# An encoder layer on one core: copy-outs moved to ScalarE, the last pair's stores moved to another queue, and the closing norm rearranged

## The chip, the cores and the metric

The kernel runs on one core of one Trainium2 chip. The metric is the device time in microseconds (us) of one execution. The kernel before was timed three times: 1658.04, 1663.20 and 1662.12 us, median 1662.12. One more execution was taken with the profiler; it lasted 1666.81 us.

## The reference, cut to what matters

One inference step of a one-layer encoder over 1024 prompt rows and 8 x 16 sample rows, D_MODEL = 1024, D_FF = 3072, all in float32. Two attention branches are merged and projected, and a gated MLP with a causal depthwise convolution of width 3 follows; RMSNorm stands before and after each of the two. The change touches the MLP alone:

```python
def conv_ffn(h, conv_buf, w_upg, conv_w, conv_b, w_down):
    u, g = jnp.split(h @ w_upg, 2, axis=-1)
    upad = jnp.concatenate([conv_buf, u], axis=1)
    c = conv_b
    for tap in range(CONV_WIDTH):
        c = c + conv_w[tap] * upad[:, tap:tap + s]
    y = (jax.nn.gelu(c, approximate=True) * g) @ w_down
    return y, upad[:, -(CONV_WIDTH - 1):]

f, conv_new = conv_ffn(rmsnorm(x, g_pre_ffn), conv_buf, w_upg, conv_w, conv_b, w_down)
x = x + rmsnorm(f, g_post_ffn)
```

rmsnorm(f, g) is f times the inverse root of the mean square of its row (plus a small constant), times the gain g of each column.

## The kernel before, in words

The 1152 rows lie in nine blocks of 128 (NT = 9). Every float32 matmul is made of three matmuls in float32r: each operand is split into a high part (a ScalarE copy, line 1007 for up weights, 1292 for the down stage) and the rest (a VectorE subtraction, lines 1008 and 1293). Around these, both stages multiply in the Strassen-Winograd way: seven products of half-sized operands in place of eight, whose results are summed in PSUM and on VectorE.

**The up stage.** There are 24 pairs f (NF = 24), each one tile of 128 u columns with its tile of g columns. The left operands of a pair are formed from its raw weights `uw` by `left_factors`; the right operands b11, b21, t3, t2, t1, b22 and t4 are tiles that stay in SBUF for the whole stage. Every product is two chunks of 288 columns (CW), 12 matmuls each, in two PSUM banks. For the first five pairs (NH = 5) the products with b11 and b21 ran ahead (`head_away`), and their results went to DRAM as a_dr and c_dr. `tail` does the rest of a pair: zb takes the product with t3, then xb the one with t2; xb is copied out into u2; the product with t1 is summed onto xb, which is copied out into u4; the product with b22 is summed onto it and xb is copied out a third time, into rows of u; last zb takes the product with t4. Since the next product is summed onto the same banks, TensorE waits for each copy-out, chunk by chunk. `take` (line 1140) is the copy-out. In the pairs run ahead a PSUM bank holds only the part made here, and `take` adds `a`, loaded back from a_dr, on VectorE (line 1144); in the others it is a ScalarE copy (line 1146). The rows of u that ran ahead are loaded from c_dr (line 1192). The convolution begins with one ScalarE instruction for each piece (line 1183: 448 columns, 128 sample columns, and 576 for the other half), then two on VectorE each (line 1185), then gelu on ScalarE (line 1187). GpSimd copies the new convolution state (lines 1202, 1203) and multiplies with the gate (1204, 1209); four stores bring the result to z_dr[f] (lines 1205, 1206, 1210, 1211). After the last pair the collected state is stored as conv_new (line 1247).

**Order of work.** A planner orders each engine's instructions by a model of their times, first those that come earlier in the program; each engine then runs its queue in that order, and an instruction that waits holds those behind it. All DMAs but none of the compute instructions stand in SyncE's queue (SP). Only where `tc.manual_schedule` names an engine is its order that of the program text.

**Memory between the stages.** The up stage's right-hand pools are uraw (the raw weights, two tiles of 8 KB a partition), b11 (18 KB), and further on t3, t2, t1, b22 and t4. The down stage lays its pools over them in the order in which they are opened: zp0 (9 KB) and wp0 (8 KB) come first and so lie over uraw, za0 and wb0 (8 KB each) over b11. zp and wp take raw loads from z_dr and w_down, za and wb the split operands. A tile waits for the last use of what it covers.

**The down stage.** The 24 tiles z_dr are multiplied with w_down in two groups g of six pairs of tiles. The first product, p2, uses the tiles of the upper half: z12 and wd12 in zp0 and wp0, then z14, z16. The sample block's columns go first in each product (p20s), with their own split (line 1299 and 1300). The sums stand in yacc, nine blocks of 1024 columns in two halves. In the second group the order at the end is written out by hand for VectorE: for each of the nine blocks the last 18 matmuls, `add_to` (line 1366) of the second half, and `finish`, a generator: x1 is loaded, ScalarE squares the block's yt and sums the squares (line 1401), GpSimd scales the sum and raises it to the power -1/2 (lines 96, 97), and, one block later, VectorE multiplies yt with that and with the gain gpo (line 1407), adds x1 (line 1410) and SyncE stores y. The ninth block is done in two halves; its two sums are added on GpSimd (line 1403), and its first half's last addition is on GpSimd.

Of the kernel before, what the change touches and what calls it, by code (L numbers as in the profile page):

```python
# [13 lines left out]
AF = mybir.ActivationFunctionType  # L14
# [4 lines left out]
P = 128  # L19
# [33 lines left out]
def encoder_step(ctx, tc, x, w_in, w_o, w_out, w_upg, w_down, kc, vc, state_conv, conv_w, conv_b,  # L53
# [40 lines left out]
    def rstd_of(ss, out, eng=nc.vector):  # L94

        eng.tensor_scalar(out, ss, 1.0 / D, EPS, op0=ALU.mult, op1=ALU.add)
        nc.gpsimd.tensor_tensor(out, out, nhalf[:, 0:out.shape[1]], op=ALU.pow)
# [986 lines left out]
    with ExitStack() as ph:  # L1084
# [55 lines left out]
        def take(xb, a, yb, out):  # L1140

            for c in range(2):
                if yb is None:
                    nc.vector.tensor_tensor(out[c], xb[c], a[c], op=ALU.add)  # L1144
                else:
                    nc.scalar.activation(out[c], xb[c], AF.Copy)
            return out

        def tail(f, ops, xb, a, yb, forms):
            zb = banks(psz, f"z{f}")  # L1150
            product(zb, next(ops), of("t3"), True, False)
            product(xb, next(ops), of("t2"), yb is None, False)
            next(forms, None)
            w = r1[f % 2].tile([P, 4 * 3 * 256], F32, name=f"w{f}", tag="act")
            u = w[:, 0:UT]
            us = u[:, UP:UT].rearrange("p (b q) -> p b q", b=NSB)
            gg = w[:, UT:UT + T].rearrange("p (h c n) -> p h c n", h=2, c=2)
            u2 = take(xb, a, yb, [w[:, UT + T + c * CW:UT + T + (c + 1) * CW] for c in range(2)])
            nc.gpsimd.memset(u[:, 0:2], 0.0)
            product(xb, next(ops), of("t1"), False, False)  # L1160
            next(forms, None)
            if "wk" not in work:
                work["wk"] = r1[2].tile([P, 4 * 3 * 256], F32, name="wk", tag="act")
                work["st"] = r1[3].tile([P, 4 * 3 * 256], F32, name="st", tag="act")
                nc.sync.dma_start(work["st"][:, 0:NF * NSB * 2].rearrange("p (f b q) -> p f b q", f=NF, b=NSB), state_conv)
            wk, st = work["wk"], work["st"]
            scv = st[:, 0:NF * NSB * 2].rearrange("p (f b q) -> p f b q", f=NF, b=NSB)
            cnew = st[:, NF * 16:NF * 34].rearrange("p (f n) -> p f n", f=NF)
            nc.gpsimd.tensor_copy(us[:, :, 0:2], scv[:, f])
            u4 = take(xb, a, yb, [wk[:, 2304 + c * CW:2304 + (c + 1) * CW] for c in range(2)])  # L1170
            for c in range(2):
                nc.vector.tensor_tensor(gg[:, 1, c], zb[c], u4[c], op=ALU.add)

            def conv(h):

# [12 lines left out]
                return c  # L1188

            for dst, c, cols, samples in rows(u, us):  # L1190
                if yb is None:
                    nc.sync.dma_start(dst, by_sample(c_dr[f][:, c, cols], samples))
                else:
                    nc.vector.tensor_tensor(dst, by_sample(yb[c][:, cols], samples), by_sample(a[c][:, cols], samples),
                                            op=ALU.add)
            c1 = conv(0)
            product(xb, next(ops), of("b22"), False, True)
            next(forms, None)
            take(xb, a, yb, [u[:, 2 + H1 + c * CW:2 + H1 + (c + 1) * CW] for c in range(2)])
            c2 = conv(1)  # L1200
            product(zb, next(ops), of("t4"), False, True)
            nc.gpsimd.tensor_copy(cnew[:, f, 0:2], u[:, SEQ:SEQ + 2])
            nc.gpsimd.tensor_copy(cnew[:, f, 2:].rearrange("p (b q) -> p b q", b=NSB), us[:, :, SS:SS + 2])
            nc.gpsimd.tensor_tensor(c2, c2, gg[:, 1].rearrange("p c n -> p (c n)"), op=ALU.mult)
            nc.sync.dma_start(z_dr[f][:, H1:512], c2[:, 0:512 - H1])
            nc.sync.dma_start(z_dr[f][:, 512 + P:T], c2[:, 512 - H1:])
            for c in range(2):
                nc.vector.tensor_tensor(gg[:, 0, c], zb[c], u2[c], op=ALU.add)
            nc.gpsimd.tensor_tensor(c1, c1, gg[:, 0].rearrange("p c n -> p (c n)"), op=ALU.mult)
            nc.sync.dma_start(z_dr[f][:, 0:H1], c1[:, 0:H1])  # L1210
            nc.sync.dma_start(z_dr[f][:, 512:512 + P], c1[:, H1:])

        def right_factors():

# [29 lines left out]
        for f in range(NF):  # L1244
            tail(f, *(head_back(f) if f < NH else head(f)), forms)
        cnew = work["st"][:, NF * 16:NF * 34].rearrange("p (f n) -> p f n", f=NF)
        nc.sync.dma_start(conv_new, cnew)
    xo_stack.close()
    r1_stack.close()

# [3 lines left out]
    with ExitStack() as ph:  # L1254
# [3 lines left out]
        def right(name):  # L1258
            return ph.enter_context(tc.tile_pool(name=name, bufs=1, side="right", reuse_waits="tile"))

        zp, wp, za, wb = [None] * 6, [None] * 6, [], []
        for q in range(3):
            zp[q], wp[q] = right(f"zp{q}"), right(f"wp{q}")
            za.append(right(f"za{q}"))
            wb.append(right(f"wb{q}"))
            if q == 0:
                yacc = right("yacc").tile([P, NT, 2, 512], F32, name="yacc")
        zsp = [right(f"zs{i}") for i in range(6)]
        for q in range(3, 6):
# [119 lines left out]
        def finish(tb, n):  # L1389

            if n % 2 == 0:
                pool = (wp + zp[3:])[3 + n // 2]
                box["x1"] = pool.tile([P, 2, D], F32, name=f"x1f{n}", tag="r")
            x1 = box["x1"][:, n % 2]
            nc.sync.dma_start(x1, x1_dr[tb][:])
            st = tp.tile([P, 4], F32, name=f"stf{tb}", tag="stf")
            sq = box["sq"][:, n % 2]
            yt = yacc[:, tb].rearrange("p a b -> p (a b)")
            parts = [slice(0, 512), slice(512, D)] if n == NT - 1 else [slice(0, D)]
            for i, c in enumerate(parts):  # L1400
                nc.scalar.activation(sq[:, c], yt[:, c], AF.Square, accum_out=st[:, i:i + 1])
            if len(parts) > 1:
                nc.gpsimd.tensor_tensor(st[:, 0:1], st[:, 0:1], st[:, 1:2], op=ALU.add)
            rstd_of(st[:, 0:1], st[:, 2:3], nc.gpsimd)
            yield
            for i, c in enumerate(parts):
                nc.vector.scalar_tensor_tensor(yt[:, c], yt[:, c], st[:, 2:3], gpo[:, c], op0=ALU.mult, op1=ALU.mult)  # L1407
            for i, c in enumerate(parts):
                eng = nc.gpsimd if n == NT - 1 and i == 0 else nc.vector
                eng.tensor_tensor(yt[:, c], yt[:, c], x1[:, c], op=ALU.add)  # L1410
                nc.sync.dma_start(y[tb][:, c], yt[:, c])

        box = {}
        pending = []

        def start_finish(tb):
            ends = finish(tb, box.setdefault("n", 0))
            box["n"] += 1
            next(ends)
            for e in pending:  # L1420
                next(e, None)
            pending[:] = [ends]

        for g in range(2):
# [44 lines left out]
            p3, n, _ = stepper("p3", pairs, xb, ex, False, False, True)  # L1469
            box["sq"] = zp[5].tile([P, 2, D], F32, name="sqf", tag="r")  # L1470
            with tc.manual_schedule(engines={mybir.EngineType.DVE}):
                add_to(xb[0], 4, 1, g, False)
                start_finish(4)
                for step, j, ps, tb in ((p5, 1, xb[1], 5), (p3, -1, ex, NT - 1), (p3, 0, xb[0], 0), (p5, 2, xb[2], 6),
                                        (p3, 1, xb[1], 1), (p5, 3, xb[3], 7), (p3, 2, xb[2], 2), (p3, 3, xb[3], 3)):
                    for i in range(n):
                        step(i, j)
                    add_to(ps, tb, 1, g, False)
                    start_finish(tb)
                for e in pending:  # L1480
                    next(e, None)

# [85 lines left out]
```

## Time and profile before

| | |
|---|---|
| timed runs, us | 1658.04, 1662.12, 1663.20 |
| profiled execution, us | 1666.81 |
| its span, first to last instruction, us | 1665.0 |
| mean granted TensorE clock | 0.991 |
| TensorE matmul, busy us | 1609.2 (97%) |
| VectorE (DVE), busy us | 1086.8 (65%) |
| ScalarE (ACT), busy us | 726.6 (44%) |
| GpSimd (POOL), busy us | 223.8 (13%) |
| DMA over SyncE's queue | 204.69 MB, 36.2% of 16 engines |

The span is what lies between the first and the last instruction; some 1.8 us of the execution lie outside. An engine is idle before an instruction when something that it needs is late; the profile names in brackets how long and what came last (the releaser). The granted clock is a share of TensorE's full 2.4 GHz. In the profile's rows PE is the matmul, PEld the weight load beside it, and a q behind an engine's name is its queue of issued DMAs or waits. The up stage runs from some 862 to 1385 us, its ahead pairs' tails until 959; the down stage follows to the end.

### The profile page before, as it was taken

The numbers are of one execution on the slowest core, as the hardware profiler recorded it, in microseconds if no ns is written. First come the engines' busy times: TensorE is split into PE (matmuls) and PEld (weight loads), VectorE is DVE, ScalarE is ACT, GpSimd is POOL, SyncE is SP. The second block draws the span as 40 slices with busy tenths as digits, with TensorE's granted clock in tenths as the row PEclk, the third lists the DMA queues.
The fourth block names the chain that finished last, engine by engine and source line by source line (L and its number), as shares of the span: only waits on it lengthen the run. The fifth ranks groups of instructions, "written<-read, shape, count | busy, mean of one in ns | idle before, by whom it ended". The sixth has DMA issues, their size and how long they took to land. (4 is left out here: it accounts for less than half of the span.)

```text
span 1665.0 us, 27771 instructions
## 1 busy us (share of the span) xinstructions
PE 1609.2 (97%) x10839; PEld 1480.8 (89%) x10839; DVE 1086.8 (65%) x2009; ACT 726.6 (44%) x1417; POOL 223.8 (13%) x297
## 2 busy tenths in 40 slices
PE   6999999999999999999999999999999998999997
PEld 6999998788888889978898999999999997888886
DVE  6965546665665546454397766766666675965986
ACT  7511235565454445332373344444444444534342
POOL 1000011111111103411002211111111110000003
PEclk9999999999999999999999999999999999999999
DMA  7743326445333236442254311221221129053023
GB/s 256 246 167 143 113 83 208 141 142 163 121 116 119 72 126 229 135 161 94 76 188 128 118 64 70 80 80 71 75 80 67 68 68 339 2 194 128 1 94 134
DMA packets 95364, 206.47 MB, mean 124 GB/s; under 512 B 21704, under 2 KB 46072, under 8 KB 95232
## 3 DMA queue, kind: packets, MB, share of 16 engines
q1 hardware_dynamic: 95232, 204.69, 36.2%
q8 instruction: 85, 1.39, 0.3%
q14 instruction: 47, 0.39, 0.1%
HBM read 148.13 MB, written 61.24 MB: 126 GB/s over the span
## 5 line engine op out<-in xcount | busy, mean ns | idle before, releaser
L143 PE MATMUL x<-xot,s 128*128 128x288 f32 x1152 | 157.7, 295 | 0.9 <-DVE w L1144 0.9
L143 PEld LDWEIGHTS x<-xot,s 128*128 128x128 f32 x1152 | 154.9, 188 | 1.1 <-ACT a L1007 1.1
L1354 PE MATMUL x<-wbp,zap 128*128 128x512 f32 x576 | 135.3, 389 | 0.0
L1354 PEld LDWEIGHTS x<-wbp,zap 128*128 128x128 f32 x576 | 108.1, 188 | 22.4
L1007 ACT ACTIVATE s<-uw 128x512 fp32r<-128x512 f32 x96 | 60.1, 626 | 96.1 <-issue 41.7
L1354 PE MATMUL p<-wbp,zap 128*128 128x512 f32 x432 | 102.0, 393 | 0.0
L1354 PEld LDWEIGHTS p<-wbp,zap 128*128 128x128 f32 x432 | 82.2, 190 | 17.2
L1008 DVE TENSOR_TENSOR s<-uw,s 128x512 fp32r<-128x512 f32 x96 | 68.9, 718 | 32.3 <-ACT s L1007 32.3
L1185 DVE SCALAR_TENSOR_TENSOR wk<-w,cw,wk 128x128 f32<-128x128 f32 (+2 forms) x144 | 83.0, 613 | 9.9 <-ACT wk L1183 9.1
L671 ACT ACTIVATE p<-p,m 128x256 f32<-128x256 f32 (+4 forms) x128 | 74.9, 588 | 33.0 <-DVE m L666 33.0
L143 PE MATMUL x<-xob,s 128*128 128x288 f32 x576 | 82.6, 299 | 6.3 <-DVE wk L1144 6.3
L143 PEld LDWEIGHTS x<-xob,s 128*128 128x128 f32 x576 | 79.6, 191 | 6.9 <-ACT s L1007 2.6
L1008 DVE TENSOR_TENSOR a<-uw,a 128x512 fp32r<-128x512 f32 x62 | 42.8, 691 | 63.6 <-ACT a L1007 62.4
L143 PE MATMUL z<-xot,s 128*128 128x288 f32 x576 | 80.7, 295 | 0.0
L143 PE MATMUL z<-xot,a 128*128 128x288 f32 x576 | 80.7, 295 | 0.0
L143 PEld LDWEIGHTS z<-xot,s 128*128 128x128 f32 x576 | 78.1, 188 | 0.0
L143 PEld LDWEIGHTS z<-xot,a 128*128 128x128 f32 x576 | 78.1, 188 | 0.0
L143 PE MATMUL ix<-t,s_i 128*128 128x288 f32 x480 | 65.6, 295 | 0.3 <-DVE iu L188 0.3
L143 PEld LDWEIGHTS ix<-t,s_i 128*128 128x128 f32 x480 | 64.3, 188 | 0.5 <-issue 0.5
L143 PE MATMUL x<-xob,a 128*128 128x288 f32 x456 | 63.9, 295 | 0.0
L143 PE MATMUL y<-xob,a 128*128 128x288 f32 x456 | 63.9, 295 | 0.0
L143 PEld LDWEIGHTS x<-xob,a 128*128 128x128 f32 x456 | 61.8, 188 | 0.0
(657 smaller groups left out, 3890.9 us busy)
## 6 DMA issues: line engine op xcount, KB each, us to landing
uw<-in_w_upg SPq DMA_DIRECT2D x53, 512.0 KB, 4.5
iw<-in_w_in SPq DMA_DIRECT2D x27, 512.0 KB, 4.6
gg<-in_dr SPq DMA_DIRECT2D x16, 576.0 KB, 3.9
in_dr<-gt SPq DMA_DIRECT2D x42, 192.0 KB, 1.9
z_dr<-wk SPq DMA_DIRECT2D x24, 256.0 KB, 2.1
z_dr<-wk SPq DMA_DIRECT2D x24, 224.0 KB, 1.9
xt<-in_x SPq DMA_DIRECT2D x9, 512.0 KB, 9.9
oT<-o_dr SPq DMA_DIRECT2D x8, 576.0 KB, 7.1
```

The lines of the kernel that those rows point to most:

```text
L143: nc.tensor.matmul(ps, w[:, i, k], right(j, c, k), start=first and n == 0, stop=last and n == len(todo) - 1, skip_group_check=True)
L671: nc.scalar.activation(p[h][:, 0:n], p[h][:, 0:n], AF.Exp, bias=least[h], scale=-1.0, accum_out=st.d[:, h, i:i + 1])
L1007: nc.scalar.activation(sp[:, 0], src, AF.Copy)
L1008: nc.vector.tensor_tensor(sp[:, 1], src, fr(sp[:, 0]), op=ALU.subtract)
L1185: nc.vector.scalar_tensor_tensor(out, src(t), cw[:, f, t:t + 1], out, op0=ALU.mult, op1=ALU.add)
L1354: nc.tensor.matmul(ps, z[:, i, k, c], w[:, j, k], start=first and n == 0, stop=last and n == 2, skip_group_check=True)
```

## The change

Five edits.

- `take` copies xb with ScalarE in every pair; in the pairs run ahead VectorE then adds `a` to the copy in SBUF.
- The four z_dr stores of the last pair, and the store of conv_new, are issued from GpSimd's queue and no longer from SyncE's.
- The pools zp0 and wp0 are opened after za0 and wb0, so that the two pairs of pools change places in memory.
- In `finish` the gain is multiplied onto yt, in place, right behind the square, in every block; mean and small constant are worked out by VectorE; GpSimd does the power alone; and one fused VectorE instruction multiplies with that and adds x1.
- `start_finish` takes the block's `add_to` as an argument. For the ninth block the first half's square and product come before that addition, and so does the end of the eighth block.

```diff
         def take(xb, a, yb, out):
             for c in range(2):
+                nc.scalar.activation(out[c], xb[c], AF.Copy)
                 if yb is None:
-                    nc.vector.tensor_tensor(out[c], xb[c], a[c], op=ALU.add)
-                else:
-                    nc.scalar.activation(out[c], xb[c], AF.Copy)
+                    nc.vector.tensor_tensor(out[c], out[c], a[c], op=ALU.add)
             return out
...
-            nc.sync.dma_start(z_dr[f][:, H1:512], c2[:, 0:512 - H1])
-            nc.sync.dma_start(z_dr[f][:, 512 + P:T], c2[:, 512 - H1:])
+            queue = nc.gpsimd if f == NF - 1 else nc.sync
+            queue.dma_start(z_dr[f][:, H1:512], c2[:, 0:512 - H1])
+            queue.dma_start(z_dr[f][:, 512 + P:T], c2[:, 512 - H1:])
...
-        nc.sync.dma_start(conv_new, cnew)
+        nc.gpsimd.dma_start(conv_new, cnew)
...
         for q in range(3):
-            zp[q], wp[q] = right(f"zp{q}"), right(f"wp{q}")
+            if q:
+                zp[q], wp[q] = right(f"zp{q}"), right(f"wp{q}")
             za.append(right(f"za{q}"))
             wb.append(right(f"wb{q}"))
             if q == 0:
+                zp[q], wp[q] = right(f"zp{q}"), right(f"wp{q}")
                 yacc = right("yacc").tile([P, NT, 2, 512], F32, name="yacc")
...
             parts = [slice(0, 512), slice(512, D)] if n == NT - 1 else [slice(0, D)]
+            if n < NT - 1:
+                yield
             for i, c in enumerate(parts):
+                if i:
+                    nc.vector.tensor_scalar(st[:, 0:1], st[:, 0:1], 1.0 / D, EPS, op0=ALU.mult, op1=ALU.add)
+                    yield
                 nc.scalar.activation(sq[:, c], yt[:, c], AF.Square, accum_out=st[:, i:i + 1])
+                nc.vector.tensor_tensor(yt[:, c], yt[:, c], gpo[:, c], op=ALU.mult)
             if len(parts) > 1:
-                nc.gpsimd.tensor_tensor(st[:, 0:1], st[:, 0:1], st[:, 1:2], op=ALU.add)
-            rstd_of(st[:, 0:1], st[:, 2:3], nc.gpsimd)
+                nc.vector.tensor_scalar(st[:, 2:3], st[:, 1:2], 1.0 / D, st[:, 0:1], op0=ALU.mult, op1=ALU.add)
+            else:
+                nc.vector.tensor_scalar(st[:, 2:3], st[:, 0:1], 1.0 / D, EPS, op0=ALU.mult, op1=ALU.add)
+            nc.gpsimd.tensor_tensor(st[:, 2:3], st[:, 2:3], nhalf[:, 0:1], op=ALU.pow)
             yield
             for i, c in enumerate(parts):
-                nc.vector.scalar_tensor_tensor(yt[:, c], yt[:, c], st[:, 2:3], gpo[:, c], op0=ALU.mult, op1=ALU.mult)
-            for i, c in enumerate(parts):
-                eng = nc.gpsimd if n == NT - 1 and i == 0 else nc.vector
-                eng.tensor_tensor(yt[:, c], yt[:, c], x1[:, c], op=ALU.add)
+                nc.vector.scalar_tensor_tensor(yt[:, c], yt[:, c], st[:, 2:3], x1[:, c], op0=ALU.mult, op1=ALU.add)
                 nc.sync.dma_start(y[tb][:, c], yt[:, c])
...
-        def start_finish(tb):
-            ends = finish(tb, box.setdefault("n", 0))
+        def start_finish(tb, add):
+            ends = finish(tb, box["n"])
+            next(ends)
+            last = box["n"] == NT - 1
             box["n"] += 1
+            if last:
+                next(pending.pop(), None)
+            add()
             next(ends)
             for e in pending:
                 next(e, None)
...
-                    add_to(ps, tb, 1, g, False)
-                    start_finish(tb)
+                    start_finish(tb, lambda: add_to(ps, tb, 1, g, False))
```

## Rows read from the trace of the kernel before

**Rows 1.** The waits of TensorE (PE) from 800 to 1420 us: what waited, for what; us in total, times, the longest.

```profile
PE x L143 <- DVE wk L1144: 6.3, 3, 2.4
PE p20s L1354 <- ACT wbp L1292: 6.0, 1, 6.0
PE x L143 <- DVE w L1144: 0.9, 1, 0.9
```

**Rows 2.** Windows of the span: stretch and its length, busy us and instructions of PE, PEld, DVE, ACT and POOL, then the granted clock, the DMA share and GB/s. The first is of pairs that were not run ahead, the second holds a wait of pair 2, the others lie around the start of the down stage.

```profile
1000.00:1200.00 200.00, 200.00 (x1502) 200.00 (x1502) 134.40 (x214) 90.94 (x180) 37.19 (x54) 1.00 0.20 72
...
915.00:922.00 7.00, 4.63 (x24) 4.62 (x24) 4.70 (x11) 1.66 (x3) 0.20 (x1) 0.76 0.49 156
...
1382.00:1385.20 3.20, 3.18 (x24) 2.94 (x23) 2.44 (x4) 1.28 (x2) 0.18 (x1) 1.00 0.94 297
1385.20:1391.00 5.80, 0.00 (x0) 0.00 (x0) 3.65 (x5) 3.22 (x5) 3.14 (x2) 0.78 0.67 245
1391.00:1393.00 2.00, 1.86 (x4) 1.49 (x5) 1.89 (x2) 1.14 (x2) 0.00 (x0) 0.50 0.93 218
1393.00:1396.00 3.00, 3.00 (x10) 2.37 (x9) 0.54 (x1) 0.00 (x0) 0.00 (x0) 0.62 0.95 347
```

**Rows 3.** The timeline in pair 1 (the second of the pairs run ahead), around the product with b22: start, us, engine, line and operation, out<-in, count, and in brackets the idle time before it and its releaser.

```profile
894.18 1.35 SPq L1192 DMA_DIRECT2D w<-c_dr  x3
...
896.82 0.76 ACT L1183 ACTIVATE wk<-w,cb,cw 128x448 f32<-128x448 f32 x1 [2.64 <-DMA w<-c_dr]
897.61 0.68 DVE L1185 SCALAR_TENSOR_TENSOR wk<-w,cw,wk 128x448 f32<-128x448 f32 x1 [2.70 <-ACT wk L1183]
898.21 0.45 DVE L1144 TENSOR_TENSOR wk<-x,a 128x288 f32<-128x288 f32 x1
...
898.81 3.43 PE L143 MATMUL x<-xob,s 128*128 128x288 f32 x24 [2.16 <-DVE wk L1144]
```

**Rows 4.** The same, at the same product of pairs 2 and 3.

```profile
915.42 1.15 ACT L1183 ACTIVATE wk<-w,cb,cw 128x448 f32<-128x448 f32 x2 [2.85 <-DMA w<-c_dr]
...
917.41 4.96 PE L143 MATMUL x<-xob,s 128*128 128x288 f32 x24 [2.37 <-DVE wk L1144]
...
935.65 1.15 ACT L1183 ACTIVATE wk<-w,cb,cw 128x448 f32<-128x448 f32 x2 [2.96 <-DMA w<-c_dr]
...
938.52 1.86 PE L143 MATMUL x<-xob,s 128*128 128x288 f32 x12 [1.75 <-DVE wk L1144]
```

**Rows 5.** The instructions of line 1146, the ScalarE copy of the other pairs: shortest, median and longest in ns, first and last start.

```profile
L1146 ACT ACTIVATE wk<-x x38: 411/412/412, 974.0 to 1378.8; 128x288 f32<-128x288 f32 x38
```

**Rows 6.** The end of the up stage: two rows of the waits of SyncE's queue from 1360 to 1400 us (columns as in rows 1), and rows of the timeline (columns as in rows 3): the last pair's product with b11, the loads for the first down product, and its start.

```profile
SPq L1283 <- DVE a L1008: 3.5, 1, 3.5
SPq L1247 <- POOL st L1202: 3.1, 1, 3.1
...
1362.62 3.36 PE L143 MATMUL x<-xob,a 128*128 128x288 f32 x24
...
1377.30 0.32 SPq L1283 DMA_DIRECT2D z12r<-z_dr  x1
...
1383.08 0.43 SPq L1284 DMA_DIRECT2D wd12r<-in_w_down  x1
...
1390.03 1.06 ACT L1292 ACTIVATE wbp<-wd12r 128x1024 fp32r<-128x1024 f32 x1 [2.33 <-DMA wd12r<-in_w_down]
...
1391.13 0.79 PE L1354 MATMUL p20s<-wbp,zs 128*128 128x512 f32 x1 [5.96 <-ACT wbp L1292]
```

**Rows 7.** The timeline of one step of the closing norm, from one block's `add_to` on.

```profile
1630.33 0.69 DVE L1366 TENSOR_TENSOR yacc<-yacc,p51s 128x512 f32<-128x512 f32 x1 [0.94 <-PE p51s L1354]
1630.93 1.28 DVE L1407 SCALAR_TENSOR_TENSOR yacc<-yacc,stf,gpo 128x1024 f32<-128x1024 f32 x1
1631.13 1.06 ACT L1401 ACTIVATE sqf<-yacc 128x1024 f32<-128x1024 f32 x1 [3.01 <-DVE yacc L1366]
1632.10 0.18 ACT L1401 ACTIVATION_READ_ACCUMULATOR sqf<-yacc 128x1 f32 x1
1632.25 1.23 DVE L1410 TENSOR_TENSOR yacc<-yacc,x1f 128x1024 f32<-128x1024 f32 x1
1632.37 1.15 POOL L96 TENSOR_SCALAR stf<-stf 128x1 f32<-128x1 f32 x1 [2.30 <-ACT sqf L1401]
```

**Rows 8.** The timeline of the stage's last part: GpSimd's first instruction in it, the last 108 matmuls, and the ninth block's end. The last row is of the groups of instructions by line and form (busy us, mean ns), a VectorE instruction on one column in an earlier stage.

```profile
1624.21 0.19 POOL L96 TENSOR_SCALAR stf<-stf 128x1 f32<-128x1 f32 x1 [235.11 <-ACT sqf L1401]
...
1630.13 24.64 PE L1354 MATMUL x<-wbp,zap 128*128 128x512 f32 x108
...
1650.73 0.69 DVE L1366 TENSOR_TENSOR yacc<-yacc,x 128x512 f32<-128x512 f32 x1 [0.94 <-PE x L1354]
...
1655.53 0.63 ACT L1401 ACTIVATE sqf<-yacc 128x512 f32<-128x512 f32 x1 [2.16 <-DVE yacc L1366]
...
1658.09 0.55 POOL L97 TENSOR_TENSOR stf<-stf,nhalf 128x1 f32<-128x1 f32 x1
1658.67 1.42 DVE L1407 SCALAR_TENSOR_TENSOR yacc<-yacc,stf,gpo 128x512 f32<-128x512 f32 x2 [0.72 <-POOL stf L97]
...
1660.12 1.63 DVE L1410 TENSOR_TENSOR yacc<-yacc,x1f 128x512 f32<-128x512 f32 x1
...
L96 DVE TENSOR_SCALAR str<-str 128x1 f32<-128x1 f32 x18 | 2.7, 152 | 28.6 <-ACT h L1056 18.8 <-ACT h L1061 9.7
```

More of the change, by code (lines that the diff above doesn't have):

```diff
@@ L1209, in tail @@
             nc.gpsimd.tensor_tensor(c1, c1, gg[:, 0].rearrange("p c n -> p (c n)"), op=ALU.mult)
-            nc.sync.dma_start(z_dr[f][:, 0:H1], c1[:, 0:H1])
-            nc.sync.dma_start(z_dr[f][:, 512:512 + P], c1[:, H1:])
+            queue.dma_start(z_dr[f][:, 0:H1], c1[:, 0:H1])
+            queue.dma_start(z_dr[f][:, 512:512 + P], c1[:, H1:])
         def right_factors():
@@ L1399, in finish @@
             parts = [slice(0, 512), slice(512, D)] if n == NT - 1 else [slice(0, D)]
+            if n < NT - 1:
+                yield
             for i, c in enumerate(parts):
+                if i:
+                    nc.vector.tensor_scalar(st[:, 0:1], st[:, 0:1], 1.0 / D, EPS, op0=ALU.mult, op1=ALU.add)
+                    yield
                 nc.scalar.activation(sq[:, c], yt[:, c], AF.Square, accum_out=st[:, i:i + 1])
+                nc.vector.tensor_tensor(yt[:, c], yt[:, c], gpo[:, c], op=ALU.mult)
             if len(parts) > 1:
-                nc.gpsimd.tensor_tensor(st[:, 0:1], st[:, 0:1], st[:, 1:2], op=ALU.add)
-            rstd_of(st[:, 0:1], st[:, 2:3], nc.gpsimd)
+                nc.vector.tensor_scalar(st[:, 2:3], st[:, 1:2], 1.0 / D, st[:, 0:1], op0=ALU.mult, op1=ALU.add)
+            else:
+                nc.vector.tensor_scalar(st[:, 2:3], st[:, 0:1], 1.0 / D, EPS, op0=ALU.mult, op1=ALU.add)
+            nc.gpsimd.tensor_tensor(st[:, 2:3], st[:, 2:3], nhalf[:, 0:1], op=ALU.pow)
             yield
             for i, c in enumerate(parts):
-                nc.vector.scalar_tensor_tensor(yt[:, c], yt[:, c], st[:, 2:3], gpo[:, c], op0=ALU.mult, op1=ALU.mult)
-            for i, c in enumerate(parts):
-                eng = nc.gpsimd if n == NT - 1 and i == 0 else nc.vector
-                eng.tensor_tensor(yt[:, c], yt[:, c], x1[:, c], op=ALU.add)
+                nc.vector.scalar_tensor_tensor(yt[:, c], yt[:, c], st[:, 2:3], x1[:, c], op0=ALU.mult, op1=ALU.add)
                 nc.sync.dma_start(y[tb][:, c], yt[:, c])
-        box = {}
+        box = {"n": 0}
         pending = []
-        def start_finish(tb):
-            ends = finish(tb, box.setdefault("n", 0))
+        def start_finish(tb, add):
+            ends = finish(tb, box["n"])
+            next(ends)
+            last = box["n"] == NT - 1
             box["n"] += 1
+            if last:
+                next(pending.pop(), None)
+            add()
             next(ends)
@@ L1471, in encoder_step @@
             with tc.manual_schedule(engines={mybir.EngineType.DVE}):
-                add_to(xb[0], 4, 1, g, False)
-                start_finish(4)
+                start_finish(4, lambda: add_to(xb[0], 4, 1, g, False))
                 for step, j, ps, tb in ((p5, 1, xb[1], 5), (p3, -1, ex, NT - 1), (p3, 0, xb[0], 0), (p5, 2, xb[2], 6),
```

## The prediction

> **What bounds the kernel now.** I read the page's busy times first: TensorE is busy for 97% of the span, so a change pays only where it closes a gap of TensorE or shortens what comes after its last matmul. The list of TensorE's waits from the up stage to the first down product then shows where the gaps are [rows 1]: 6.3 us in three waits for line 1144, the copy-out on VectorE of the pairs run ahead, 0.9 us in one more such wait, and 6.0 us in one wait for a down weight's split. In the 200 us of pairs that are not run ahead TensorE never stops [rows 2]. The same windows show that a gap costs more than its length: after one of the 2.4 us the granted clock over 7 us was 0.76, and after the 6 us it was 0.50 and 0.62 over 5 us [rows 2]; 0.50 is the lower of the two levels, 1.2 GHz. The last matmul ends at 1630.13 + 24.64 = 1654.77, and VectorE's last instruction at 1661.75 [rows 8]: 7.0 us of tail. The sum goes against the profiled execution, 1666.81 us (span 1665.0 and 1.8 around it); that lies 4.7 us above the median of 1662.12, to which I then apply the difference.
>
> **Part A, copies by ScalarE.** For five pairs each of three copy-outs becomes two ScalarE copies and two VectorE adds that read SBUF. VectorE's count is the same (0.45 us each [rows 3]); ScalarE gets 6 x 0.41 = 2.5 us a pair [rows 5] and even in the stretch of pairs whose copies were its own already it was busy 91 of 200 us [rows 2]. TensorE now waits for the copy and no longer for the add. What that is worth depends on what stands ahead of the copy in ScalarE's queue. In pair 1 VectorE's add was late since it stood behind line 1185, which waited for ScalarE's line 1183, which waited for the load of c_dr issued at 894.18; the chain ended with the add at 898.21 and TensorE at 898.81 [rows 3]. So ScalarE was held by the same load until 896.82. Two bounds:
> - Copies ahead of line 1183 in all three pairs: all 6.3 us go, and the 1.5 us that the 24 matmuls of pair 2 took longer at the lower clock (4.96 against 3.43 us [rows 3, 4]). Gain 7.8.
> - Copies behind both instructions of line 1183. In pair 2 these end at 915.42 + 1.15 = 916.57, the copy at 916.98, against a restart at 917.41: 0.4 saved. In pair 3 the first half is also held, until 937.2, and the product ends at some 940.45 against 938.52 + 1.86 = 940.38: nothing saved [rows 4]. Gain, with the same spread for pair 1, -0.5 to 0.5, without the clock.
>
> I take the middle. The planner put line 1185 ahead of the add, so its model had line 1183 ready a little earlier than the first copy; but ScalarE now also has two copies before that, and the copy belongs to the earlier pair than the second piece does. So: one instruction of 1183 ahead of the copy in pairs 1 and 2. Pair 1: 896.82 + 0.68 + 0.41 = 897.9 against 898.81, 0.9 saved; pair 2: 915.42 + 0.6 + 0.41 = 916.45, 1.0 saved; pair 3: the half that waited restarts at 936.3 + 0.45 = 936.8 to 937.2 against 938.52, 1.3 saved. 3.2, and with stalls then below the one that was followed by the lower clock, 1.5 for it: 4.7. For the 0.9 us I count nothing.
>
> **Part B, the start of the down stage.** TensorE ended the up stage at 1391.13 - 5.96 = 1385.17 and waited for the split of wd12, whose second load was issued only at 1383.08 [rows 6]. Two things held it. z12's load waited for the last split out of the raw up weights, 3.5 us, until 1377.30; and SyncE's queue stood 3.1 us at the conv_new store, which waited for GpSimd's line 1202, with the weight loads behind it [rows 6]. The change takes away both. zp0 and wp0 now lie where b11 lay, and the last product that reads b11 ended at 1362.62 + 3.36 = 1365.98: the first four loads can go some 9 us earlier, at 1368 to 1370, behind the previous pair's stores. What takes over the raw weights' place are the split operands za0 and wb0, free at 1377.3. Splits of 4 x some 1.1 us on each of two engines end near 1383, before 1385.17. The sample columns' split (0.4 us) has the place of b22, free only at 1382; it is the next late thing, and I leave 0.5 us for it and for VectorE's queue there. The stores and conv_new go to GpSimd, which has nothing to do for 235 us afterwards [rows 8]; z_dr of the last pair is read in the second group of the down stage, some 100 us on. A store's issue from GpSimd is in no row; between SyncE's 0.3 us and several us it delays nobody. So 5.5 us of the gap go, and the slow restart with it: 15 matmuls of 0.23 took from 1391.13 to 1396.4, 5.3 against 3.4 us, another 1.8. Gain 7.3; bounds 3.5 (below) and 7.8.
>
> The Trainium skill (DMA: Bandwidth & Descriptors, "Issuing engines are not separate DMA queues") says that DMAs started by different engines run on the same 16 DMA engines, and that spreading them saves only the sequencer's issue time. By that rule the new queue gives no bandwidth, and where the gap is one of bytes the move is worth nothing. The row speaks for bytes at one place, DMA share 0.94 in the last 3.2 us before the gap; that is a rival below.
>
> **Part C, the final norm.** The square reads yt on ScalarE, and the new product with the gain writes yt in place on VectorE: so it must wait for the square, and VectorE, in its written order, waits with it. A step of VectorE now is: add to start of square 0.80, square and its accumulator 1.15, handover 0.05, product 1.13 (1.23, next 0.09 before its end, as the add of 0.69 hands over after 0.60), the tensor_scalar some 0.10 (0.15 long), the fused last step of the block before 1.19: 4.42 us [rows 7, 8]. TensorE's step is 4.08 (add at 1630.33, next one step on). VectorE was ahead before; now it falls back 0.34 us a step, from the second block to the eighth 6 x 0.34 = 2.0. The eighth add starts at 1650.73 + 2.0 = 1652.8. Then a period of 4.42, half a product 0.60, a tensor_scalar 0.10 and the eighth block's last step 1.19 come ahead of the ninth add: 1659.1, where before it followed the last matmul at once. From there: 0.80, half a square 0.73 [rows 8], 0.05, half a product 0.60, tensor_scalar and handover 0.20, power 0.55, 0.03, two halves 1.42: 4.4, so 1663.5 against 1661.75. The early product saves GpSimd's three instructions and the late add, some 2.5 us behind the last add, but the last add comes 4.3 later. Loss 1.7. Bounds: if nothing accumulates, 1661.4, a gain of 0.35; if the power of the eighth block also waits for VectorE, as GpSimd's line 96 took 1.15 beside a VectorE instruction and 0.19 alone [rows 7, 8], 0.6 to 1 more: loss 2.7.
>
> **Sum.** 4.7 + 7.3 - 1.7 = 10.3. Profile 1656.5, span 1654.7; on the median 1651.8.
>
> **Rivals.**
> - ScalarE takes over VectorE's wait: both pieces of line 1183 stand before the copies, part A gives 0 and the clock drops again. For it: the same load is the root, and nothing in the diff loads it earlier. Against it: two more copies compete in ScalarE. Gain 5.6, 1656.5.
> - The gap at the down stage is one of bytes. In the 3.2 us before it the core's DMA ran at 0.94 and 297 GB/s [rows 2]; two sets of loads (4.4 MB) from 1368 on would take 15 us, to 1383, and with splits 1386.5 to 1388, and the clock drops for part of it. Part B gives 3.5 to 4, total 6.6, 1655.5. Against it: the first set alone is 2.2 MB, 7.6 us.
> - The other side: ScalarE's order puts line 1183 of the next pair ahead of the copy after the second product too. Then the third product, which starts near 893.4 in pair 1, would wait for 897.5 + 0.41 or for the second piece, 4.5 to 5.5 us where it lost 2.16. In three pairs some 3.4 more each, 10.3, and the clock falls in each, 3 us more: 13.3 lost against 5.6 won, 7.7 slower, 1669.8. It decides where the planner's model has c_dr landed before the second product ends. Against it: VectorE's order has both adds after that product ahead of line 1185 in all these pairs.
> - The last part does what it says: the products overlap the squares, VectorE keeps up, and the tail is 0.35 shorter: 12.4 won, 1649.7.
>
> **Chances.** Forecast 0.55, ScalarE's wait 0.17, bytes 0.10, the better tail 0.10, slower side 0.06, none of these and within a few us of before 0.02. A measurement here can tell 0.3%, 5 us, from no change. Faster by that: the forecast, the better tail, most of the bytes' case and about half of ScalarE's, with some off each for errors of the sum: 0.76; within it 0.17; slower 0.07. Range: from a gain of 15.1 (A and B whole, the tail even) to 2.6 (A nothing, B at its lower bound with a tail of -1.7 gives 1.8; a little is left out): 1647.0 to 1659.5.
>
> **What would show it.** TensorE's waits for line 1144 gone, and waits for the copy under 1.5 us each, or none, in their place, with the clock at 1.0 over all ahead pairs. SyncE's z12 and wd12 loads at 1368 to 1370 on the old scale, and the first down matmul within 1 us of the last up matmul, at clock 1.0. VectorE idle 1.1 to 1.3 us a step before the new product, its adds later by some 0.3 a step, the ninth add 4 us after the last matmul. I am wrong if ScalarE is found waiting for c_dr with a copy behind it, if the first down product waits for a load, or if the tail is not longer than 7.0 us.

## The result and the profile after

The changed kernel takes 1668.11 us in the median of eight runs (1663.30 to 1670.09), the kernel before 1660.89 in eight runs beside them (1656.72 to 1664.41). The ratio is 1.0036, 95% interval 1.0022 to 1.0049: slower by some 6 us by the ratio (7.2 by the medians), where 10 us faster was forecast. The profiled execution of the changed kernel took 1669.32 us, with a span of 1667.5.

Three stretches tell where it went. S1 runs from the first tail product of the pairs run ahead to the first product of pair 5, S2 from the end of the last up matmul to the end of the last matmul, S3 from there to the end of the span. All three are read off the timeline's matmul rows and the span. The kernels of the experiments leave one part or another as it was, so that the scatter of unchanged code is known as well (the number of profiles stands in brackets).

| stretch, us | before, profiled | all profiles with that part unchanged | changed kernel |
|---|---|---|---|
| S1, copies | 89.7 | 87.1 to 89.9, mean 88.4 (7) | 91.4 |
| S2, down stage | 269.6 | 267.2 to 270.5, mean 268.8 (6) | 269.7 |
| S3, tail | 10.2 | 10.1 to 10.3 (6) | 12.9 |

Against those means the three parts cost 3.0, 0.9 and 2.7 us: 6.6, against the 6 of the runs. A single profile scatters, though. Four more kernels below hold the copies as the changed kernel does, and with its own their S1 is 90.4 to 91.9, mean 91.0: a cost of 2.5. Four hold its closing norm, and with its own their S3 is 12.3 to 12.9, mean 12.5: a cost of 2.3.

TensorE's waits after, from 860 to 1430 us (columns as in [rows 1]; the lines behind 1143 have moved a little).

```profile
PE x L143 <- ACT wk L1143: 7.8, 4, 3.7
PE p10s L1356 <- ACT yacc L1366: 2.8, 1, 2.8
PE p20s L1356 <- ACT zs L1301: 0.9, 1, 0.9
PE p20s L1356 <- DVE zs L1302: 0.7, 1, 0.7
PE p L1356 <- DVE w L1208: 0.6, 1, 0.6
```

The 6.3 and 0.9 us of [rows 1] did not go: where they were 7.2 in four waits they are 7.8 in four now, and the releaser is the new copy on ScalarE. The one wait of 6.0 us became four of 0.6 to 2.8.

Pairs 1 and 2 after, where [rows 3, 4] stood before (timeline; line 1191 is the load of c_dr, 1182 the first convolution instruction).

```profile
891.64 1.34 SPq L1191 DMA_DIRECT2D w<-c_dr  x3
...
894.26 0.76 ACT L1182 ACTIVATE wk<-w,cb,cw 128x448 f32<-128x448 f32 x1 [2.29 <-DMA w<-c_dr]
...
895.90 0.49 ACT L1182 ACTIVATE wk<-w,cb,cw 128x128 f32<-128x128 f32 x1 [0.89 <-DMA w<-c_dr]
896.30 0.69 ACT L1143 ACTIVATE wk<-x 128x288 f32<-128x288 f32 x2
...
896.74 3.46 PE L143 MATMUL x<-xob,s 128*128 128x288 f32 x24 [2.55 <-ACT wk L1143]
...
915.83 0.49 ACT L1182 ACTIVATE wk<-w,cb,cw 128x128 f32<-128x128 f32 x1 [1.82 <-DMA w<-c_dr]
...
916.67 5.98 PE L143 MATMUL x<-xob,s 128*128 128x288 f32 x24 [3.67 <-ACT wk L1143]
```

ScalarE waits for the next pair's c_dr, runs both pieces of its convolution's start, and only then the two copies that TensorE stands for. In pair 2 the 24 matmuls behind the wait took 5.98 us in place of 3.46, where [rows 4] has 4.96; the granted clock over them was 0.52. So of the 1.7 us between the two profiles of S1 0.6 are waits and 1.0 are these slower matmuls.

The start of the down stage after, where [rows 6] stood. First the waits of SyncE's queue around it:

```profile
SPq L1285 <- DMA z_dr<-wk: 7.1, 1, 7.1
SPq L1286 <- DMA out<-st: 5.5, 1, 5.5
```

The second line is the store of conv_new. That wait was over at 1390.8, before the last pair's stores were issued (1391.1 on), so it does not set when z2, below, can be loaded. Then the row of the DMA issues for the largest of the last pair's four stores (the last column is us from issue to landing; the same store from SyncE has a median of 2.1 over the other 23 pairs), and a row of the page's DMA queues (packets, MB, share of 16 engines):

```profile
z_dr<-wk POOLq DMA_DIRECT2D x1, 256.0 KB, 6.9
```

```profile
q0 software_dynamic: 272, 0.81, 0.1%
```

The 0.81 MB are the five stores that moved. They stand in a queue of another kind, which the page of before does not have; what SyncE issues stands in q1, hardware_dynamic.

And the timeline:

```profile
1368.01 0.40 SPq L1285 DMA_DIRECT2D z12r<-z_dr  x1
...
1385.75 0.73 PE L1356 MATMUL p20s<-wbp,zs 128*128 128x512 f32 x2 [0.86 <-ACT zs L1301]
...
1392.76 0.54 POOL L1211 DMA_DIRECT2D z_dr<-wk  x1
...
1399.47 0.32 SPq L1285 DMA_DIRECT2D z2r<-z_dr  x1
...
1407.69 0.42 ACT L1301 ACTIVATE zs<-z2r 128x256 fp32r<-128x256 f32 x1 [7.44 <-DMA z2r<-z_dr]
...
1409.91 0.58 ACT L1366 ACTIVATE yacc<-p20s 128x512 f32<-128x512 f32 x1
...
1411.03 1.65 PE L1356 MATMUL p10s<-wbp,zs 128*128 128x512 f32 x3 [2.76 <-ACT yacc L1366]
```

The early loads came as forecast (z12 at 1368.01, the down stage some 0.9 us after the last up matmul). But the last pair's stores, issued by GpSimd until 1393.3, landed only at 1399.4. The load of z2 goes over the tile that they read, so SyncE's queue stood 7.1 us for it; ScalarE stood 7.4 us for z2, with the copy-outs of the first product queued behind; and the second product found no free PSUM bank for 2.8 us. Over the 2 us behind that wait the granted clock was 0.50.

The tail after: one step of VectorE, and the ninth block's end (compare [rows 7, 8]).

```profile
1630.36 0.68 DVE L1368 TENSOR_TENSOR yacc<-yacc,p51s 128x512 f32<-128x512 f32 x1
...
1632.34 1.23 DVE L1410 TENSOR_TENSOR yacc<-yacc,gpo 128x1024 f32<-128x1024 f32 x1 [1.30 <-ACT sqf L1409]
...
1634.74 0.68 DVE L1368 TENSOR_TENSOR yacc<-yacc,x 128x512 f32<-128x512 f32 x1
...
1656.81 0.63 ACT L1409 ACTIVATE sqf<-yacc 128x512 f32<-128x512 f32 x1 [2.61 <-DVE yacc L1418]
...
1659.43 0.68 DVE L1368 TENSOR_TENSOR yacc<-yacc,x 128x512 f32<-128x512 f32 x1
...
1662.47 1.41 DVE L1418 SCALAR_TENSOR_TENSOR yacc<-yacc,stf,x1f 128x512 f32<-128x512 f32 x2 [0.75 <-POOL stf L1415]
```

From add to add it is 4.38 us. VectorE stands some 1.30 us in each step for the square, and the ninth add starts 4.85 us after the last matmul (1654.58).

### The profile page after: what moved, and what is told of

Read it like the earlier page. It is cut to its first block, busy times and chain, and to the rows that moved or that the text cites. A ratio compares the mean times of both kernels' runs of the same rounds, so it can differ in the third digit from the quotient of the medians.

```text
span 1667.5 us, 27794 instructions
## 1 busy us (share of the span) xinstructions
PE 1610.6 (97%) x10839; PEld 1480.9 (89%) x10839; DVE 1087.3 (65%) x2020; ACT 735.6 (44%) x1447; POOL 223.2 (13%) x291
## 4 chain that ended last, share of the span: by engine, by line
PE 85%; DVE 5%; DMA 5%; ACT 2%; issue 2%; POOL 1%; SPq 0%; DVEq 0%; POOLq 0%; ACTq 0%
PE x L143 16%; PE z L143 9%; PE ix L143 6%; PE x L1356 5%; PE p L1356 5%; PE y L143 4%; PE iz L143 4%; PE d L117 4%; PE d L119 3%; PE d L118 3%; PE pt L703 3%; PE s L663 3%; PE o L718 2%; PE r L1048 2%; PE mp L915 2%; PE mp L916 2%
## 5 line engine op out<-in xcount | busy, mean ns | idle before, releaser
L1184 DVE SCALAR_TENSOR_TENSOR wk<-w,cw,wk 128x448 f32<-128x448 f32 (+2 forms) x144 | 83.4, 614 | 10.7 <-ACT wk L1182 10.0
L1143 ACT ACTIVATE w<-x 128x288 f32<-128x288 f32 x96 | 39.6, 412 | 86.0 <-PE x L143 86.0
```

## The experiments

**One part alone.** Each is the kernel before with one part of the change. a_only:

```diff
+                nc.scalar.activation(out[c], xb[c], AF.Copy)
                 if yb is None:
-                    nc.vector.tensor_tensor(out[c], xb[c], a[c], op=ALU.add)
-                else:
-                    nc.scalar.activation(out[c], xb[c], AF.Copy)
+                    nc.vector.tensor_tensor(out[c], out[c], a[c], op=ALU.add)
```

> The kernel before with the copies by ScalarE alone. My theory: ScalarE runs both pieces of the next pair's first convolution instruction, which wait for the load of c_dr, ahead of the copy that TensorE needs. Then from the first tail product to the first product of pair 5 it takes 91.4 us (before 89.7, changed kernel 91.4), TensorE waits 7 to 9 us for the copies, and the whole is 1 to 2 us slower. Rival (the copies help, and the loss comes from the other parts, which shift the planner's order): 85 to 87 us, 3 to 5 us faster.

S1 was 91.9 us, with 7.7 us of waits for the copies; ratio 1.0007 (0.9991 to 1.0022). As my theory had it in the stretch; the whole is too small a difference to tell.

pool_only:

```diff
-            zp[q], wp[q] = right(f"zp{q}"), right(f"wp{q}")
+            if q:
+                zp[q], wp[q] = right(f"zp{q}"), right(f"wp{q}")
             za.append(right(f"za{q}"))
             wb.append(right(f"wb{q}"))
             if q == 0:
+                zp[q], wp[q] = right(f"zp{q}"), right(f"wp{q}")
```

> The kernel before with zp0 and wp0 behind za0 and wb0 alone; all stores stay on SyncE. From the last up matmul to the last matmul it took 269.6 us before and 269.7 in the changed kernel. My theory: the early loads close most of the gap, and what gave it back are the stores on GpSimd's queue; then 263 to 266 us, no wait of the second down product above 0.5 us, 4 to 6 us faster. Rival: ScalarE's order puts splits that wait for loads ahead of the copy-outs whatever the queue; then 268 to 270 us and no gain.

S2 was 266.3 us, just outside the forecast, with no wait in the second product; ratio 0.9973 (0.9961 to 0.9986), 4.5 us faster, of which S2 shows 2.5 beside the mean of 268.8. So this part is a gain by itself, though the start kept waits of 1.2, 0.7 and 0.6 us, with a granted clock of 0.62 over the 3.8 us behind them.

queue_only:

```diff
-            nc.sync.dma_start(z_dr[f][:, H1:512], c2[:, 0:512 - H1])
+            queue = nc.gpsimd if f == NF - 1 else nc.sync
+            queue.dma_start(z_dr[f][:, H1:512], c2[:, 0:512 - H1])
...
-        nc.sync.dma_start(conv_new, cnew)
+        nc.gpsimd.dma_start(conv_new, cnew)
```

> The kernel before with the last pair's four stores and conv_new on GpSimd's queue alone. My theory: SyncE gets past conv_new, the second load of wd12 goes some 3.5 us earlier, and the first wait shrinks from 6.0 to 2 to 3 us; but the stores land 6 us after issue in place of 3, the loads laid over their source tiles go later, and a wait of 1 to 4 us comes in the second down product: 267 to 270 us from the last up matmul to the last matmul. Rival: the queue of the stores is no cost, 264 to 266 us.

S2 was 267.3 us; the first wait was still 3.7, as in two of the kernels that leave this part alone, and there was no wait in the second product: half a miss. The stores landed 5.9 to 6.7 us after their issue here too, and SyncE stood 6.6 us for them. But in this kernel ScalarE's first copy-out stood ahead of z2's split. Ratio 0.9993 (0.9983 to 1.0003).

c_only is the change's `finish` and `start_finish` alone; its core:

```diff
                 nc.scalar.activation(sq[:, c], yt[:, c], AF.Square, accum_out=st[:, i:i + 1])
+                nc.vector.tensor_tensor(yt[:, c], yt[:, c], gpo[:, c], op=ALU.mult)
...
-                nc.vector.scalar_tensor_tensor(yt[:, c], yt[:, c], st[:, 2:3], gpo[:, c], op0=ALU.mult, op1=ALU.mult)
...
+                nc.vector.scalar_tensor_tensor(yt[:, c], yt[:, c], st[:, 2:3], x1[:, c], op0=ALU.mult, op1=ALU.add)
```

> The kernel before with the closing norm's edit alone. My theory: VectorE waits for each square, a step takes 4.38 us against TensorE's 4.08, and the last add comes 4.8 us after the last matmul; from the last matmul to the end of the span 12.9 us (before 10.2), 2 to 3 us slower as a whole. Rival: the tail of the changed kernel comes from the shifted loads before it; then 10 to 11 us.

S3 was 12.5 us; ratio 1.0011 (0.9999 to 1.0022). The tail belongs to this part; the whole is too small a difference to tell.

**Is it the order on ScalarE?** a_order is a_only with a rule for the planner: what pair f + 1 issues on ScalarE for its convolution's first half is queued behind pair f's second copies.

```diff
+                copied["last"] = nc.scalar.activation(out[c], xb[c], AF.Copy)
...
+            before = copied.get("u4")
             u4 = take(xb, a, yb, [wk[:, 2304 + c * CW:2304 + (c + 1) * CW] for c in range(2)])
+            copied["u4"] = copied["last"]
...
-            c1 = conv(0)
+            if yb is None and before is not None:
+                with tc.issue_after(before.ins if hasattr(before, "ins") else before):
+                    c1 = conv(0)
+            else:
+                c1 = conv(0)
```

> The copies by ScalarE as in a_only, with one thing more: the next pair's first convolution instructions (the two that wait for c_dr) are queued behind this pair's second copies. My theory: that order alone is what cost; TensorE's waits for the copies go, and from the first tail product to the first product of pair 5 it takes 81 to 83 us (a_only 91.9, before 89.7). Rival (the copy plus the later convolution delays something else in the pair): 86 us or more.

S1 was 80.1 us, a little under the forecast: all waits of the stretch are gone, 8 us less than with the adds and 11.8 less than a_only. Ratio 0.9956 (0.9940 to 0.9972). The rows of pair 1's third product and ScalarE around it (line 1145 is the copy, 1186 the convolution):

```profile
890.03 0.41 ACT L1145 ACTIVATE wk<-x 128x288 f32<-128x288 f32 x1 [0.67 <-PE x L143]
...
891.43 3.36 PE L143 MATMUL x<-xob,s 128*128 128x288 f32 x24
891.63 0.41 ACT L1145 ACTIVATE wk<-x 128x288 f32<-128x288 f32 x1 [1.19 <-PE x L143]
...
892.46 1.14 ACT L1186 ACTIVATE wk<-w,cb,cw 128x448 f32<-128x448 f32 x2
```

The copies go as soon as TensorE is through, and the convolution's start finds its load landed: it waits for nothing. The order was not tried with the adds left on VectorE, so how much of the 8 us needs the copies as well stays open.

**Which store, which queue?** all_sync is the changed kernel with both edits of queue_only taken back.

> The changed kernel with the last pair's stores and conv_new back on SyncE's queue. My theory: the wait in the second down product came of the stores' late landing from GpSimd, so it goes: from the last up matmul to the last matmul 266 to 267 us (pool_only 266.3, changed kernel 269.7), and the whole is 3 us faster than the changed kernel, within 0.2% of before. Rival (the wait comes from the planner's order with all parts together): 269 to 270 us.

S2 was 264.7 us, 5.0 less than in the changed kernel and below the forecast, and the wait in the second product 0.8. Ratio to before 1.0016 (1.0002 to 1.0030), so some 3 us better than the changed kernel as a whole, though the two intervals overlap. Two more kernels take back one of the two; each was executed once. stores_gp is the changed kernel with

```diff
-        nc.gpsimd.dma_start(conv_new, cnew)
+        nc.sync.dma_start(conv_new, cnew)
```

> The changed kernel with conv_new back on SyncE; the four stores stay on GpSimd. If the landing of the stores is what delays the second set of loads (z2) and with it ScalarE's copy-outs, the wait of the second down product is there, 2 to 3 us, and the stretch from the last up to the last matmul takes 268 to 270 us. If conv_new's store is, 264 to 266 us.

and conv_gp the changed kernel with

```diff
-            queue = nc.gpsimd if f == NF - 1 else nc.sync
-            queue.dma_start(z_dr[f][:, H1:512], c2[:, 0:512 - H1])
-            queue.dma_start(z_dr[f][:, 512 + P:T], c2[:, 512 - H1:])
+            nc.sync.dma_start(z_dr[f][:, H1:512], c2[:, 0:512 - H1])
+            nc.sync.dma_start(z_dr[f][:, 512 + P:T], c2[:, 512 - H1:])
...
```

> The changed kernel with the four stores back on SyncE; conv_new stays on GpSimd. By the first theory no wait above 1 us in the second down product, 264 to 266 us; by the other 268 to 270 us.

With the stores on GpSimd S2 was 268.3 and the wait 2.5 us; with conv_new there, 264.1 and no such wait. It is the move of the stores. In stores_gp the row of the DMA issues for the same store:

```profile
z_dr<-wk POOLq DMA_DIRECT2D x1, 256.0 KB, 6.6
```

The waits of SyncE's queue there:

```profile
SPq L1285 <- DMA z_dr<-wk: 10.4, 2, 10.3
```

And TensorE's wait in the timeline:

```profile
1409.04 1.64 PE L1356 MATMUL p10s<-wbp,zs 128*128 128x512 f32 x3 [2.48 <-ACT yacc L1366]
```

In all_sync the same store of 256 KB landed 2.1 us after its issue.

The late landing is not the whole of it. ScalarE's order is another one too. In stores_gp it splits z2 and wd2 whole before the first copy-out (line 1366):

```profile
1405.71 0.42 ACT L1301 ACTIVATE zs<-z2r 128x256 fp32r<-128x256 f32 x1 [7.74 <-DMA z2r<-z_dr]
1406.03 1.04 ACT L1294 ACTIVATE zap<-z2r 128x1024 fp32r<-128x1024 f32 x1
1406.98 1.04 ACT L1294 ACTIVATE wbp<-wd2r 128x1024 fp32r<-128x1024 f32 x1
1407.92 0.58 ACT L1366 ACTIVATE yacc<-p20s 128x512 f32<-128x512 f32 x1
```

In all_sync only the short first split stands ahead of it (lines 1300 and 1365 there):

```profile
1404.95 0.42 ACT L1300 ACTIVATE zs<-z2r 128x256 fp32r<-128x256 f32 x1 [4.83 <-DMA z2r<-z_dr]
1405.27 0.58 ACT L1365 ACTIVATE yacc<-p20s 128x512 f32<-128x512 f32 x1
```

The last up matmul ends at 1383.62 in stores_gp and at 1383.94 in all_sync. Counted from there, z2's split starts 1.1 us later in stores_gp and the copy-out 3.0 us later; the other 1.9 are the two long splits. (Against conv_gp it is 3.6 and 3.8.) So moving the stores costs through the landing and through the planner's order that comes with it; no run here takes the two apart.

**What was left of the gap?** layout_only lays out the down stage's pools anew, on the kernel before.

```diff
+        def raw_pools(q):
+            zp[q], wp[q] = right(f"zp{q}"), right(f"wp{q}")
+
+        def operand_pools(q):
             za.append(right(f"za{q}"))
             wb.append(right(f"wb{q}"))
...
+        operand_pools(0)
+        raw_pools(0)
+        raw_pools(3)
+        zsp = [right(f"zs{i}") for i in range(6)]
+        for q in (1, 2):
+            raw_pools(q)
+            operand_pools(q)
+        yacc = right("yacc").tile([P, NT, 2, 512], F32, name="yacc")
+        for q in (4, 5):
+            raw_pools(q)
```

> The kernel before with the down stage's pools laid out anew: split operands of the first set over the raw weights, then its raw loads over b11, then pools that are used late, the sample splits over b21, which is free 16 us before the up stage ends, and yacc over b22 and t4. My theory: what was left of the gap in pool_only (1.2 + 0.7 + 0.6 us and a slow clock) came of the sample splits' late place; then TensorE goes from the up to the down stage with less than 1 us of waits and takes 261.6 to 263.5 us from the last up matmul to the last matmul. Rival (ScalarE's order is not a matter of that place): 266 us.

S2 was 261.5 us, at the low end of the forecast; ratio 0.9969 (0.9954 to 0.9984). In the profile the last up product and the first down product follow each other without a wait:

```profile
1378.11 3.36 PE L143 MATMUL z<-xot,a 128*128 128x288 f32 x24
1381.31 2.02 PE L1363 MATMUL p20s<-wbp,zs 128*128 128x512 f32 x8
```

**The tail's order.** c_order has the VectorE instructions of c_only in another order: `start_finish` runs the block before between the square and the product that waits for it, and the ninth add is not held by the eighth block's end. Against c_only:

```diff
                 nc.scalar.activation(sq[:, c], yt[:, c], AF.Square, accum_out=st[:, i:i + 1])
+                if i == len(parts) - 1:
+                    yield
                 nc.vector.tensor_tensor(yt[:, c], yt[:, c], gpo[:, c], op=ALU.mult)
...
-            last = box["n"] == NT - 1
             box["n"] += 1
-            if last:
-                next(pending.pop(), None)
             add()
             next(ends)
             for e in pending:
                 next(e, None)
+            next(ends)
             pending[:] = [ends]
```

> The closing norm's edit with the same instructions in another order on VectorE: the add, then the fused last step of the block before, and only then the new product that waits for the square; and the ninth add ahead of the eighth block's last step. My theory: the wait for the square is filled, a step is TensorE's 4.08 us again, the ninth add follows the last matmul at once, and from the last matmul to the end of the span it takes 7.5 to 8.5 us (before 10.2, c_only some 12.5). Rival (VectorE's work is simply too long for a step): 11 us or more.

S3 was 8.0 us, 4.4 less than c_only and 2.2 less than before. One step:

```profile
1637.68 0.69 DVE L1366 TENSOR_TENSOR yacc<-yacc,x 128x512 f32<-128x512 f32 x1 [0.80 <-PE x L1354]
1638.29 1.28 DVE L1418 SCALAR_TENSOR_TENSOR yacc<-yacc,stf,x1f 128x1024 f32<-128x1024 f32 x1
...
1639.67 1.23 DVE L1410 TENSOR_TENSOR yacc<-yacc,gpo 128x1024 f32<-128x1024 f32 x1
...
1641.76 0.69 DVE L1366 TENSOR_TENSOR yacc<-yacc,x 128x512 f32<-128x512 f32 x1 [0.81 <-PE x L1354]
```

The step is 4.08 again, and it is VectorE that waits for TensorE. The runs alone would not have shown it: ratio 0.9992 (0.9979 to 1.0006).

c_stf3 gives the column of sums three buffers: `tag="stf", bufs=3`.

> c_only with three buffers in place of two for the column of sums. In the changed kernel the ninth block's first square started only when the seventh block's last step had ended. If the two buffers are the cause, it now starts right behind the eighth block's square, and the stretch from the last matmul to the end of the span is 0.8 to 1.0 us shorter than c_only's 12.5. If ScalarE's order is the cause, no change.

S3 was 11.5 in the one execution, 0.9 less than c_only. In c_only the ninth block's first square waited for the fused step:

```profile
1651.08 0.63 ACT L1407 ACTIVATE sqf<-yacc 128x512 f32<-128x512 f32 x1 [2.61 <-DVE yacc L1416]
```

In c_stf3 it started right behind the eighth's, whose sum is the first row:

```profile
1645.39 0.19 ACT L1407 ACTIVATION_READ_ACCUMULATOR sqf<-yacc 128x1 f32 x1
1645.48 0.61 ACT L1407 ACTIVATE sqf<-yacc 128x512 f32<-128x512 f32 x1
```

**Together.** best_a is a_order, layout_only and c_order in one, all stores on SyncE.

> The three repaired parts together, all stores on SyncE: a_order, layout_only and c_order. If the three stages add up, 80 to 82 us for the ahead pairs' tails, 261.5 to 262.5 us from the last up to the last matmul and 8.0 us of tail: 12 to 16 us faster than before, a ratio of 0.990 to 0.993. Rival (the planner's order shifts with all parts together, as it did in the changed kernel): 0.994 or more.

1644.47 us in the median of four runs, beside 1661.52 of the kernel before: ratio 0.9899 (0.9882 to 0.9915), 17 us faster, a little beyond the forecast. S1 80.0, S2 262.4, S3 8.0. Its windows (columns as in [rows 2]) for the three stretches, the gap between the stages in the third row:

```profile
865.00:946.00 81.00, 81.00 (x610) 81.00 (x609) 74.87 (x128) 45.20 (x85) 20.95 (x28) 1.00 0.45 138
946.00:1371.00 425.00, 424.60 (x3185) 424.37 (x3184) 285.97 (x455) 195.67 (x383) 78.09 (x112) 1.00 0.23 83
1371.00:1376.00 5.00, 4.63 (x21) 3.29 (x21) 3.91 (x6) 2.03 (x4) 1.53 (x2) 1.00 0.71 240
1376.00:1634.00 258.00, 257.99 (x1138) 213.14 (x1136) 204.74 (x216) 103.87 (x126) 5.61 (x10) 1.00 0.31 116
```

Against the means of the table the stages gain 8.4, 6.4 and 2.2 us, 17.0 together: they add up, and the clock is granted in full in all four windows.

## Why the prediction was wrong

- **What bounds the kernel** held: TensorE's gaps and the tail are all that moved the time, and best_a gains by closing just these.
- **Part A, taken at 4.7 gained; it cost 2.0 to 3.4 in five profiles, 2.5 in the mean.** The step that failed is "I take the middle. ... one instruction of 1183 ahead of the copy in pairs 1 and 2". Both pieces went ahead (895.90 before 896.30), which was my lower bound, and even that was too mild: in pair 2 the second piece's load landed at 915.8, so the wait was 3.7 us and not the some 2 that the row of before gave, and the clock fell to 0.52 behind it. The first rival had the mechanism; it priced part A at nothing, and it cost. That the order is what cost, a_order shows: with it the copies gain 8 us, my upper bound.
- **Part B, taken at 7.3; it gave none.** The early loads came as forecast. Three things failed. "It delays nobody", said of the stores on GpSimd, was wrong: I looked for readers of z_dr and not for the loads that lie over the stores' source tile. conv_gp and stores_gp put it on the stores, and the rows of ScalarE add that its order changed with them. The 0.5 us left for the sample splits and VectorE's queue was 2.1 in three waits (in pool_only 2.4, with the lower clock behind); layout_only, which gives the sample splits a place that is free earlier and moves other pools too, has none of them. And the gap of 6.0 us on which the sum rests was at its long end: in six profiles of kernels that have that part unchanged it is 3.7 to 6.0.
- **The bytes' rival** fell: on the same transfers all_sync starts the down stage with waits of 0.5 and 0.7 us and layout_only with none. The Trainium skill (DMA: Bandwidth & Descriptors, "Issuing engines are not separate DMA queues") says that another queue saves only issue time. The trace agrees that it saved nothing here: S2 is 264.1 us with conv_new moved (conv_gp) and 264.7 with nothing moved (all_sync), a difference within the scatter.
- **Part C, taken at 1.7 lost, measured 2.1 to 2.7.** The mechanism was right: a step of 4.38 against the 4.42 worked out, VectorE idle 1.30 in each. The missing term is the wait of the ninth block's first square for the seventh block's last step, 0.9 us, from the two buffers of the column of sums (c_stf3). The better-tail rival needed another order (c_order).
- **The other side** was priced as one rival, ScalarE ahead of the second product's copies. Slower came instead from A and B both ending below the lower bounds that I gave them (A -0.5, measured -2.0 to -3.4; B 3.5, measured about nothing), with C, which the sum had as a loss already. The chances treated these as apart; in both, part of what went wrong was the order in one engine's queue, where work that waits for a load stood ahead of work that TensorE waits for.

What stays open: why the stores issued by GpSimd land later, and why the planner put z2's and wd2's splits ahead of all copy-outs in the changed kernel and stores_gp but not in queue_only or all_sync. Neither was tried.

## What to carry to other kernels

When a wait is moved to another engine, read what that engine's queue holds ahead of the new instruction: if that waits for the same load, the wait may only change its place. Here writing the order down turned a loss of 2.5 us into a gain of 8. When a store changes its queue, ask which loads reuse its source tile, and not only who reads its target, and read the order of the other engines again. A product formed early in place must wait for whoever still reads its operand; fill that wait with the block before.

## What the runs showed of the hardware

The last pair's stores (32 to 256 KB), issued by GpSimd, landed 5.9 to 6.9 us after their issue in the three kernels that have them there; SyncE's, of the same sizes, have medians of 1.4 to 2.1 over a kernel, and 2.7 to 3.0 for the last pair in the kernel before. For the 256 KB alone it is 6.6 to 6.9 against 2.1 and 3.0. Little of it goes with the size: GpSimd's 32 KB took 5.9 to 6.2. conv_new (216 KB) took 5.5 to 6.2 us from GpSimd and 2.8 to 5.1 from SyncE. The issue itself took 0.54 to 0.77 us of GpSimd, against 0.32 to 0.43 on SyncE.

The Trainium skill (DMA: Bandwidth & Descriptors, "Anatomy of one DMA — SWDGE (gpsimd) path") gives some 2.0 us and the bytes at 436 GB/s for a DMA issued by GpSimd, an estimate of 2.6 us for 256 KB. The measurement decides: it is longer by 4 us.
